# Early rows of w_up: the last two products exchanged, the spilled first product as one fp32 tile, and pools at 256-byte steps

## The chip, the cores and the metric

The kernel runs on one core of a Trainium2 chip. The metric is the device time of one execution, in microseconds; lower is better. TensorE does the matrix products, ACT (ScalarE) and DVE (VectorE) move results from PSUM to SBUF and do elementwise work, POOL (GpSimd) does small work and issues DMAs, and SP (SyncE) only issues DMAs.

## The reference

One decoder layer on 1024 tokens of width 1024, in float32: parallel token mixers, cross-attention to 256 memory tokens, and a gated MLP with a causal convolution of width 3. The change touches the first half of the MLP, and the places of tiles everywhere.

```python
h += W_out(g_A * P_A(n) + g_B * P_B(n))            # n = RMSNorm(h)
h += CrossAttn(RMSNorm(h), RMSNorm(mem))
h += W_down(silu(conv(u)_gate) * conv(u)_val)      # u = W_up RMSNorm(h), 2816 + 2816 columns
```

## The kernel before

A product of high precision is made of three fp32r products: each operand is split into a rounded part (hi) and its rest (lo), and hi x hi, hi x lo and lo x hi are summed in PSUM (`mm3`, L97). The split is one ACT copy and one DVE subtraction (`split_to`, L81; `hilo`, L103, from PSUM).

u = W_up n is computed for 22 rows of 128 columns, each a gate half and a value half, for the two halves of the tokens. One row is a 2 x 2 block product by Strassen's scheme in Winograd's form, seven products in place of eight. A product (`product`, L812) is four blocks of 128 times three, twelve matmuls of 128 x 512. The right operands are "11", "21" and "22" and the sums t1 to t4, all split once; the left operands are a row's weights w1 and w2 (raw tiles wr and w), of which only l22 is used as it is, and the sums s1 to s4, made on DVE by `sum_weights` (L920) and split into tiles mh and ml with two buffers each.

A row is made by three functions. `up_start` (L895) allocates ug and uv (gate and value rows before the convolution; tag hu, two buffers, so each row takes the buffers of the row before), opens bank A and puts the first product into it. `up_middle` (L936) adds s2 x t2 to A and copies it out (U2, L948), makes s3 x t3 in bank B, adds s1 x t1 to A and copies that out (U4, L953), and writes B plus U4 into the second half of uv. `up_end` (L956) has the last two products: c12, s4 x R22 added to A, which is then copied to ug (L958); and c21, l22 x t4 added to B, which is written with U2 into the first half of uv (L960). `add_into` (L916) is an ACT copy (L917) and a DMA on POOL's queue that adds a tile in place (L918). Then both rows go through the convolution (ACT L966, DVE L967 and L968), SiLU and product; of odd rows, six halves and sums are written to r_d for the last stage.

The rows stand in a pipeline: for each g, `up_start(g)`, `up_end(g - 1)`, `up_middle(g)`. Ten of the 22 rows are early rows (NEARLY = 10): their products with "11" and "21" are made beforehand by `up_early` (L827), since only the first half of the tokens is needed for them. It makes the first product P1, stores it as a split pair in er_d, adds the second and stores the sum in e_d. Row g then loads the pair by two DMAs on POOL's queue (L904, L905) and puts both into bank A with an identity matrix in fp32r (`ident_r`, copied at L166; L906, L907); the stored sum is loaded straight into the first half of ug by SP (L940). The other twelve rows, the late rows, make all seven products in place.

Each engine's order of work is set by a planner in the framework: it goes through the instructions by the time it believes them ready, and the order of the text is the tie-break. Engines work through their own order one after the other; POOL's and SP's DMAs are issued in theirs.

Tiles live in pools: cp, bp and the tag pools (ug, uv, y, h, weights wr, wh, wl, activations a2h, a2l, and the e tiles that `etile` takes) on the left, ap, xp, mp, tp and dn on the right of SBUF. The tiles neghalf and ident_r (cp), rs8 (L168), rsm (L699) and ncw (L1087) have widths that set where the others begin.

Of the kernel before, what the change touches and what calls it, by code (L numbers as in the profile page):

```python
# [7 lines left out]
F32 = mybir.dt.float32  # L8
F32R = mybir.dt.float32r
AF = mybir.ActivationFunctionType  # L10
# [4 lines left out]
P = 128  # L15
T = 1024
D = 1024
NK = D // P
HT = 512
# [17 lines left out]
NEARLY = 10  # L37
# [5 lines left out]
def hybrid_layer(ctx: ExitStack, tc: tile.TileContext, x, xT, mem, memT, w_in, w_v, w_br, w_out, w_xq, w_xk, w_xv, w_xo, w_up,  # L43
                 w_down, vecs, ln_f, consts, tabs, out):
    nc = tc.nc

    cp = ctx.enter_context(tc.tile_pool(name="cp", bufs=1))
# [3 lines left out]

    ident = cp.tile([P, P], F32, name="ident")
    vec = cp.tile([P, V_N], F32, name="vec")
    neghalf = cp.tile([P, 16], F32, name="neghalf")
    ident_r = cp.tile([P, P + 16], F32R, name="ident_r")[:, :P]

    ga_d = dp.tile([16, P, T], F32, name="ga_d")
    yt_d = dp.tile([6, P, T], F32, name="yt_d")
# [1 line left out]
    rs_d = dp.tile([T], F32, name="rs_d")  # L60
    sd_d = dp.tile([NF // 2, P, 4, HT], F32, name="sd_d")
    r_d = dp.tile([NF // 2, 7, P, HT], F32, name="r_d")
    e_d = dp.tile([NEARLY, P, HT], F32, name="e_d")
    er_d = dp.tile([NEARLY, 2, P, HT], F32R, name="er_d")
    h_d = dp.tile([8, P, D], F32, name="h_d")

    def f(ap):
# [35 lines left out]
    def hilo(hi, lo, ps, scale=None):  # L103
        if scale is None:
            nc.scalar.activation(hi, ps, AF.Copy)
            nc.vector.tensor_tensor(lo, ps, f(hi), op=ALU.subtract)
        else:
            nc.scalar.activation(hi, ps, AF.Copy, scale=scale)
            nc.vector.scalar_tensor_tensor(lo, ps, scale, f(hi), op0=ALU.mult, op1=ALU.subtract)
# [53 lines left out]
            hilo(nT[h][0][:, k], nT[h][1][:, k], xt[:, h * HT:(h + 1) * HT], vec[:, V_MIX + k:V_MIX + k + 1])  # L163

    nc.sync.dma_start(ident, consts[:, 0:P])
    nc.scalar.activation(ident_r, ident, AF.Copy)  # L166
    nc.sync.dma_start(cst, consts[:, P:])
    rs8 = ap.tile([P, 16], F32, name="rs8")[:, 0:8]  # L168
    for t in range(8):
        xk = ap.tile([P, D], F32, tag="kg", name="xk", bufs=4)  # L170
        nc.sync.dma_start(xk, x[t * P:(t + 1) * P, :])
# [497 lines left out]
    def etile(name, dt=F32):  # L669
        return ep.tile([P, HT], dt, tag="e", name=name, bufs=7)  # L670
# [17 lines left out]
    def mem_prep():  # L688
        KT = KV["k"] = (slot([P, 4, MEM], F32R, "kth"), slot([P, 4, MEM], F32R, "ktl"))
        VM = KV["v"] = (slot([P, 2, HT], F32R, "vmh"), slot([P, 2, HT], F32R, "vml"))  # L690
        mh = [slot([P, 4, MEM], F32R, "mh") for _ in range(2)]
        ml = [slot([P, 4, MEM], F32R, "ml") for _ in range(2)]
        for c in range(2):
            mr = slot([P, 4, MEM], F32, "mr")
            nc.gpsimd.dma_start(mr, memT[c])
            for kk in range(4):
                g = V_MEM + 4 * c + kk
                hilo(mh[c][:, kk], ml[c][:, kk], mr[:, kk], vec[:, g:g + 1])
        rsm = xp.tile([P, 18], F32, name="rsm")[:, :2]  # L699
        for t in range(2):  # L700
            mt = slot([P, D], F32, "mt")
            nc.gpsimd.dma_start(mt, mem[t * P:(t + 1) * P, :])
            nc.scalar.activation(mt, mt, AF.Square, accum_out=rsm[:, t:t + 1])
        nc.vector.tensor_scalar(rsm, rsm, 1.0 / D, EPS, op0=ALU.mult, op1=ALU.add)
        rstd(rsm, 2)
        rbm = slot([P, MEM], F32, "rbm")
        nc.vector.tensor_copy(rbm, row_bcast(rsm, 2)[:, :MEM])
        KV["m"] = mh, ml, rsm, rbm
# [103 lines left out]
    def product(ps, w, r, first):  # L812
        for kk in range(4):
            ks = slice(kk * P, (kk + 1) * P)
            mm3(ps, (w[0][:, ks], w[1][:, ks]), (r[0][:, kk], r[1][:, kk]), first and kk == 0, kk == 3,
                skip_group_check=True)
# [4 lines left out]
    R = {}  # L821
# [5 lines left out]
    def up_early(gs):  # L827
        ps = {}
        for g in gs:
            ps[g] = bank("mm", 3, "pe"), *gate_weights(g)  # L830
            product(ps[g][0], ps[g][1], R["11"], True)
            hi, lo = etile("phi", F32R), etile("plo", F32R)
            hilo(hi, lo, ps[g][0])
            nc.gpsimd.dma_start(er_d[g, 0], hi)
            nc.gpsimd.dma_start(er_d[g, 1], lo)
        for g in gs:
            product(ps[g][0], ps[g][2], R["21"], False)
            c11 = etile("c11")
            nc.scalar.activation(c11, ps[g][0], AF.Copy)
            nc.gpsimd.dma_start(e_d[g], c11)  # L840

    def spill_h(t):
        nc.gpsimd.dma_start(h_d[t], h[t])
# [51 lines left out]
    def up_start(g):  # L895
        u = {}
        u["ug"], u["uv"] = (htile([P, 2 + T + 14], "hu", n) for n in ("ug", "uv"))
        u["A"] = bank("zz", 2, "pA")
        u["w1"] = raw_w(w_up[g])
        u["w2"] = htile([P, 2 * HT], "hr", "w2")  # L900
        nc.sync.dma_start(u["w2"], w_up[NF + g])
        if g < NEARLY:
            hi, lo = etile("phi", F32R), etile("plo", F32R)
            nc.gpsimd.dma_start(hi, er_d[g, 0])  # L904
            nc.gpsimd.dma_start(lo, er_d[g, 1])  # L905
            nc.tensor.matmul(u["A"], ident_r, hi, start=True, stop=False, skip_group_check=True)  # L906
            nc.tensor.matmul(u["A"], ident_r, lo, start=False, stop=True, skip_group_check=True)  # L907
        else:
            hi, lo = split(u["w1"])
            u["l12"] = hi[:, HT:], lo[:, HT:]  # L910
            product(u["A"], (hi[:, :HT], lo[:, :HT]), R["11"], True)
            u["p1"] = etile("p1")
            nc.scalar.activation(u["p1"], u["A"], AF.Copy)
        return u

    def add_into(dst, ps, x):  # L916
        nc.scalar.activation(dst, ps, AF.Copy)  # L917
        nc.gpsimd.dma_start(dst, x, accum_op=ALU.add)  # L918
# [17 lines left out]
    def up_middle(g, u):  # L936
        for n in ("ug", "uv"):
            nc.gpsimd.memset(u[n][:, 0:2], 0.0)
        if g < NEARLY:
            nc.sync.dma_start(u["ug"][:, 2:2 + HT], e_d[g])  # L940
        else:
            d = bank("mm", 3, "pD")
            product(d, u["l12"], R["21"], True)
            add_into(u["ug"][:, 2:2 + HT], d, u["p1"])
        s1, s2, s3, u["s4"] = sum_weights(u)
        product(u["A"], s2, R["t2"], False)
        u["U2"] = etile("U2")
        nc.scalar.activation(u["U2"], u["A"], AF.Copy)  # L948
        u["B"] = bank("tr", 2, "pB")
        product(u["B"], s3, R["t3"], True)  # L950
        product(u["A"], s1, R["t1"], False)
        u4 = etile("U4")
        nc.scalar.activation(u4, u["A"], AF.Copy)  # L953
        add_into(u["uv"][:, 2 + HT:2 + T], u["B"], u4)

    def up_end(g, u):  # L956
        product(u["A"], u["s4"], R["22"], False)
        nc.scalar.activation(u["ug"][:, 2 + HT:2 + T], u["A"], AF.Copy)  # L958
        product(u["B"], u["l22"], R["t4"], False)
        add_into(u["uv"][:, 2:2 + HT], u["B"], u["U2"])  # L960
        ys = []
        for n, cw, cb, sign in (("ug", vec, V_CB + g, 0), ("uv", ncw, V_CB + NF + g, 1)):
            c0 = 3 * g if sign else V_CW + 3 * g
# [120 lines left out]
    mp = ctx.enter_context(tc.tile_pool(name="mp", bufs=1, side="right"))  # L1084
    ts_ = ExitStack()
    tp_ = ts_.enter_context(tc.tile_pool(name="tp", bufs=1, side="right"))
    ncw = mp.tile([P, 160], F32, name="ncw")  # L1087
    nc.vector.tensor_scalar(ncw[:, :3 * NF], vec[:, V_CW + 3 * NF:V_CW + 6 * NF], -1.0, None, op0=ALU.mult)
    right_sums(b12, b22)
    before = None  # L1090
# [89 lines left out]
```

## Time and profile before

| | us |
|---|---|
| median of three runs | 1780.95 |
| lowest and highest | 1777.82 and 1784.14 |
| the profiled execution | 1780.45 |
| its span | 1778.6 |
| TensorE busy | 1693.4 |
| DVE busy | 1113.0 |
| ACT busy | 871.0 |
| POOL busy | 326.9 |

The profile is one execution; its mean granted TensorE clock is 0.986 of full speed. The engine rows overlap, so they do not add up to the span. `up_early` and the set-up of the right operands end near 1149 us; the early rows run until about 1298 us, the late rows until 1550, the last stage until the end. Matmuls overlap in the records, so the distance between starts tells the pace better than a matmul's own length.

### The profile page before, as it was taken

How to read it: one execution, taken by the hardware profiler on the slowest of the kernel's cores; microseconds unless marked ns; L12 is line 12 of the kernel's file. 1: busy time of each engine (PE TensorE's matmuls, PEld its weight loads, DVE VectorE, ACT ScalarE, POOL GpSimd, SP SyncE). 2: the span in 40 equal slices, each digit the busy share in tenths (PEclk: the TensorE clock that was granted, in tenths of full speed). 3: DMA queues.
4: the chain of work that ended last, by engine and by line, in shares of the span. 5: the costliest groups of instructions: out<-in, count | busy, mean ns of one | idle time of the engine just before them, and what ended most of it. 6: DMA issues, size and time to landing. Idle time of an engine off the chain costs nothing.

```text
span 1778.6 us, 23614 instructions
## 1 busy us (share of the span) xinstructions
PE 1693.4 (95%) x8598; PEld 1378.1 (77%) x8598; DVE 1113.0 (63%) x1737; ACT 871.0 (49%) x1495; POOL 326.9 (18%) x511
## 2 busy tenths in 40 slices
PE   7999999998999899999999989798999999989997
PEld 5977777878878787788888767576778888778885
DVE  3764654468757466575645666777777767655556
ACT  5344544466345445444534455454555555534344
POOL 0442333221112110001000102222222222200002
PEclk9999999999999999999999999899999999999999
DMA  7443333455774843566322325666755454677664
GB/s 305 113 123 92 107 83 84 134 134 145 200 140 118 159 113 95 180 181 249 131 95 72 130 83 178 206 165 184 211 148 157 136 136 125 188 259 231 214 191 140
DMA packets 106388, 273.01 MB, mean 153 GB/s; under 512 B 16096, under 2 KB 16352, under 8 KB 106272
## 3 DMA queue, kind: packets, MB, share of 16 engines
q1 hardware_dynamic: 66368, 166.68, 28.9%
q0 software_dynamic: 39904, 104.82, 24.1%
q8 instruction: 68, 1.11, 0.3%
q14 instruction: 48, 0.39, 0.1%
HBM read 188.77 MB, written 74.29 MB: 148 GB/s over the span
## 4 chain that ended last, share of the span: by engine, by line
PE 66%; issue 13%; DMA 10%; DVE 5%; ACT 3%; POOL 3%; SPq 0%; POOLq 0%; DVEq 0%; ACTq 0%
PE mm L99 4%; PE mm L101 4%; PE mm L100 4%; PE pA L99 3%; PE pA L100 3%; PE pA L101 3%; DMA sd_d<-in_w_down_dram 2%; DMA uv<-U 2%; PE mmt L99 2%; PE dA L100 2%; PE dA L101 2%; PE mmt L100 2%; PE mmt L101 2%; PE dA L99 2%; DMA xw<-xs 2%
## 5 line engine op out<-in xcount | busy, mean ns | idle before, releaser
L101 PE MATMUL mm<-a2h,wl 128*128 128x512 f32 x592 | 235.2, 398 | 0.0
L99 PE MATMUL mm<-a2h,wh 128*128 128x512 f32 x592 | 234.7, 396 | 0.0
L100 PE MATMUL mm<-a2l,wh 128*128 128x512 f32 x592 | 234.5, 396 | 0.0
L83 DVE TENSOR_TENSOR wl<-wr,wh 128x1024 fp32r<-128x1024 f32 (+1 forms) x119 | 145.3, 1222 | 95.0 <-ACT wh L82 92.1
L82 ACT ACTIVATE wh<-wr 128x1024 fp32r<-128x1024 f32 (+1 forms) x119 | 124.0, 1043 | 132.6 <-PE mmt L101 29.2
L83 DVE TENSOR_TENSOR dl<-rl,dh 128x1024 fp32r<-128x1024 f32 x77 | 94.1, 1224 | 85.0 <-ACT dh L82 81.5
L82 ACT ACTIVATE dh<-rl 128x1024 fp32r<-128x1024 f32 x77 | 81.2, 1058 | 114.6 <-PE dA L101 41.2
L101 PEld LDWEIGHTS mm<-a2h,wl 128*128 128x128 f32 x592 | 112.4, 190 | 22.2 <-issue 1.0
L100 PEld LDWEIGHTS mm<-a2l,wh 128*128 128x128 f32 x592 | 112.3, 190 | 22.3 <-issue 0.9
L99 PEld LDWEIGHTS mm<-a2h,wh 128*128 128x128 f32 x592 | 112.5, 190 | 22.0 <-issue 0.9
L493 DVE TENSOR_TENSOR_SCAN kp<-kp 128x128 f32<-128x128 f32 (+7 forms) x64 | 86.8, 1356 | 29.4 <-ACT kp L490 29.1
L99 PE MATMUL pA<-a2h,mh 128*128 128x512 f32 x176 | 70.5, 400 | 14.9 <-ACT U L953 14.9
L502 ACT ACTIVATE at<-tra 128x512 f32<-128x512 f32 (+3 forms) x96 | 43.3, 489 | 76.9 <-PE tra L500 59.6
L112 POOL TENSOR_TENSOR ss<-ss,neghalf 128x1 f32<-128x1 f32 x24 | 23.3, 995 | 307.6 <-DVE ss L597 305.7
L490 ACT ACTIVATE kp<-zz,zsc 128x512 f32<-128x512 f32 (+3 forms) x96 | 55.6, 583 | 49.3 <-DVE zz L489 44.5
L381 ACT ACTIVATE sp<-sp,nm 128x128 f32<-128x128 f32 (+1 forms) x96 | 42.3, 442 | 72.6 <-DVE nm L379 72.5
L100 PE MATMUL dA<-dl,dh 128*128 128x512 f32 x176 | 70.1, 398 | 3.5 <-DVE dl L83 3.5
L101 PE MATMUL dA<-dh,dl 128*128 128x512 f32 x176 | 70.0, 397 | 0.0
L101 PE MATMUL pA<-a2h,ml 128*128 128x512 f32 x176 | 69.3, 394 | 0.0
L100 PE MATMUL pA<-a2l,mh 128*128 128x512 f32 x176 | 69.3, 394 | 0.0
L99 PE MATMUL dA<-dh 128*128 128x512 f32 x176 | 62.1, 393 | 3.8 <-ACT dh L82 3.8
L491 ACT ACTIVATE gg<-zz,zsc 128x512 f32<-128x512 f32 (+3 forms) x96 | 55.7, 583 | 7.1 <-DVE gg L494 7.1
(352 smaller groups left out, 4587.4 us busy)
## 6 DMA issues: line engine op xcount, KB each, us to landing
rl<-r_d SPq DMA_DIRECT2D x77, 256.0 KB, 3.2
wr<-in_w_in_dram SPq DMA_DIRECT2D x37, 512.0 KB, 4.2
wr<-in_w_up_dram SPq DMA_DIRECT2D x32, 512.0 KB, 4.3
w<-in_w_up_dram SPq DMA_DIRECT2D x22, 512.0 KB, 3.7
uv<-U POOLq DMA_DIRECT2D x44, 256.0 KB, 4.7
r_d<-ts POOLq DMA_DIRECT2D x44, 256.0 KB, 4.8
rl<-sd_d SPq DMA_DIRECT2D x44, 256.0 KB, 3.6
r_d<-y POOLq DMA_DIRECT2D x33, 256.0 KB, 3.4
```

What stands on the lines that cost most here:

```text
L82: nc.scalar.activation(hi, raw, AF.Copy)
L83: nc.vector.tensor_tensor(lo, raw, f(hi), op=ALU.subtract)
L99: nc.tensor.matmul(ps, wh, rh, start=first, stop=False, **kw)
L100: nc.tensor.matmul(ps, wh, ro, start=False, stop=False, **kw)
L101: nc.tensor.matmul(ps, wo, rh, start=False, stop=last, **kw)
L112: nc.gpsimd.tensor_tensor(ss, ss, neghalf[:, :n], op=ALU.pow)
L381: nc.scalar.activation(sp[:, a, :n], sp[:, a, :n], AF.Exp, scale=0.125, bias=nm[:, a:a + 1], accum_out=ost[:, 130 + a:131 + a])
L490: nc.scalar.activation(kp[:, c0:c1], z[:, :n], AF.Sigmoid, scale=zsc[:, 1, i:i + 1])
L491: nc.scalar.activation(gg[:, c0:c1], z[:, :n], AF.Sigmoid, scale=zsc[:, 0, i:i + 1])
L493: nc.vector.tensor_tensor_scan(rev, rev, rev, 1.0, op0=ALU.mult, op1=ALU.bypass)
L502: nc.scalar.activation(s[:, :nb * P], tp[:, :nb * P], AF.Copy)
```

## The change

- In `up_end`, c21 and its evacuation stand before c12 and its evacuation as long as the next row is an early row (g + 1 < 10).
- `up_early` stores P1 as one fp32 tile (one ACT copy, one DMA on POOL's queue). Row g loads it by one DMA on SP's queue and puts it into bank A with one fp32 matmul with `ident`. `ident_r` and its copy go, and er_d becomes a second plane of e_d.
- neghalf, rs8, rsm and ncw get wider by 16 or 32 elements.

```diff
--- before.py
+++ after.py
@@ -51,8 +51,7 @@
 
     ident = cp.tile([P, P], F32, name="ident")
     vec = cp.tile([P, V_N], F32, name="vec")
-    neghalf = cp.tile([P, 16], F32, name="neghalf")
-    ident_r = cp.tile([P, P + 16], F32R, name="ident_r")[:, :P]
+    neghalf = cp.tile([P, 32], F32, name="neghalf")
 
     ga_d = dp.tile([16, P, T], F32, name="ga_d")
     yt_d = dp.tile([6, P, T], F32, name="yt_d")
@@ -60,8 +59,7 @@
     rs_d = dp.tile([T], F32, name="rs_d")
     sd_d = dp.tile([NF // 2, P, 4, HT], F32, name="sd_d")
     r_d = dp.tile([NF // 2, 7, P, HT], F32, name="r_d")
-    e_d = dp.tile([NEARLY, P, HT], F32, name="e_d")
-    er_d = dp.tile([NEARLY, 2, P, HT], F32R, name="er_d")
+    e_d = dp.tile([NEARLY, 2, P, HT], F32, name="e_d")
     h_d = dp.tile([8, P, D], F32, name="h_d")
 
     def f(ap):
@@ -163,9 +161,8 @@
             hilo(nT[h][0][:, k], nT[h][1][:, k], xt[:, h * HT:(h + 1) * HT], vec[:, V_MIX + k:V_MIX + k + 1])
 
     nc.sync.dma_start(ident, consts[:, 0:P])
-    nc.scalar.activation(ident_r, ident, AF.Copy)
     nc.sync.dma_start(cst, consts[:, P:])
-    rs8 = ap.tile([P, 16], F32, name="rs8")[:, 0:8]
+    rs8 = ap.tile([P, 48], F32, name="rs8")[:, 0:8]
     for t in range(8):
         xk = ap.tile([P, D], F32, tag="kg", name="xk", bufs=4)
         nc.sync.dma_start(xk, x[t * P:(t + 1) * P, :])
@@ -696,7 +693,7 @@
             for kk in range(4):
                 g = V_MEM + 4 * c + kk
                 hilo(mh[c][:, kk], ml[c][:, kk], mr[:, kk], vec[:, g:g + 1])
-        rsm = xp.tile([P, 18], F32, name="rsm")[:, :2]
+        rsm = xp.tile([P, 50], F32, name="rsm")[:, :2]
         for t in range(2):
             mt = slot([P, D], F32, "mt")
             nc.gpsimd.dma_start(mt, mem[t * P:(t + 1) * P, :])
@@ -829,15 +826,14 @@
         for g in gs:
             ps[g] = bank("mm", 3, "pe"), *gate_weights(g)
             product(ps[g][0], ps[g][1], R["11"], True)
-            hi, lo = etile("phi", F32R), etile("plo", F32R)
-            hilo(hi, lo, ps[g][0])
-            nc.gpsimd.dma_start(er_d[g, 0], hi)
-            nc.gpsimd.dma_start(er_d[g, 1], lo)
+            p1 = etile("p1")
+            nc.scalar.activation(p1, ps[g][0], AF.Copy)
+            nc.gpsimd.dma_start(e_d[g, 0], p1)
         for g in gs:
             product(ps[g][0], ps[g][2], R["21"], False)
             c11 = etile("c11")
             nc.scalar.activation(c11, ps[g][0], AF.Copy)
-            nc.gpsimd.dma_start(e_d[g], c11)
+            nc.gpsimd.dma_start(e_d[g, 1], c11)
 
     def spill_h(t):
         nc.gpsimd.dma_start(h_d[t], h[t])
@@ -900,11 +896,9 @@
         u["w2"] = htile([P, 2 * HT], "hr", "w2")
         nc.sync.dma_start(u["w2"], w_up[NF + g])
         if g < NEARLY:
-            hi, lo = etile("phi", F32R), etile("plo", F32R)
-            nc.gpsimd.dma_start(hi, er_d[g, 0])
-            nc.gpsimd.dma_start(lo, er_d[g, 1])
-            nc.tensor.matmul(u["A"], ident_r, hi, start=True, stop=False, skip_group_check=True)
-            nc.tensor.matmul(u["A"], ident_r, lo, start=False, stop=True, skip_group_check=True)
+            p1 = etile("p1")
+            nc.sync.dma_start(p1, e_d[g, 0])
+            nc.tensor.matmul(u["A"], ident, p1, start=True, stop=True, skip_group_check=True)
         else:
             hi, lo = split(u["w1"])
             u["l12"] = hi[:, HT:], lo[:, HT:]
@@ -937,7 +931,7 @@
         for n in ("ug", "uv"):
             nc.gpsimd.memset(u[n][:, 0:2], 0.0)
         if g < NEARLY:
-            nc.sync.dma_start(u["ug"][:, 2:2 + HT], e_d[g])
+            nc.sync.dma_start(u["ug"][:, 2:2 + HT], e_d[g, 1])
         else:
             d = bank("mm", 3, "pD")
             product(d, u["l12"], R["21"], True)
@@ -954,10 +948,16 @@
         add_into(u["uv"][:, 2 + HT:2 + T], u["B"], u4)
 
     def up_end(g, u):
-        product(u["A"], u["s4"], R["22"], False)
-        nc.scalar.activation(u["ug"][:, 2 + HT:2 + T], u["A"], AF.Copy)
-        product(u["B"], u["l22"], R["t4"], False)
-        add_into(u["uv"][:, 2:2 + HT], u["B"], u["U2"])
+        def c12():
+            product(u["A"], u["s4"], R["22"], False)
+            nc.scalar.activation(u["ug"][:, 2 + HT:2 + T], u["A"], AF.Copy)
+
+        def c21():
+            product(u["B"], u["l22"], R["t4"], False)
+            add_into(u["uv"][:, 2:2 + HT], u["B"], u["U2"])
+
+        for part in (c21, c12) if g + 1 < NEARLY else (c12, c21):
+            part()
         ys = []
         for n, cw, cb, sign in (("ug", vec, V_CB + g, 0), ("uv", ncw, V_CB + NF + g, 1)):
             c0 = 3 * g if sign else V_CW + 3 * g
@@ -1084,7 +1084,7 @@
     mp = ctx.enter_context(tc.tile_pool(name="mp", bufs=1, side="right"))
     ts_ = ExitStack()
     tp_ = ts_.enter_context(tc.tile_pool(name="tp", bufs=1, side="right"))
-    ncw = mp.tile([P, 160], F32, name="ncw")
+    ncw = mp.tile([P, 192], F32, name="ncw")
     nc.vector.tensor_scalar(ncw[:, :3 * NF], vec[:, V_CW + 3 * NF:V_CW + 6 * NF], -1.0, None, op0=ALU.mult)
     right_sums(b12, b22)
     before = None
```

## Rows read from the trace of the kernel before

**Rows 1.** Windows, early and late rows: length, busy time by engine (instructions), clock, DMA share, GB/s.
```profile
1164.50:1297.50 133.00, 118.13 (x496) 93.55 (x495) 100.42 (x109) 72.63 (x90) 38.77 (x75) 0.99 0.66 189
...
1303.00:1545.00 242.00, 242.00 (x1053) 197.37 (x1052) 177.68 (x183) 133.82 (x173) 59.28 (x106) 1.00 0.52 139
```
**Rows 2.** Waits, 1148 to 1303 us: us in total, times, longest.
```profile
ACT y L966 <- DMA uv<-U: 15.1, 7, 3.9
...
PE pA L99 <- ACT U L953: 14.9, 8, 3.2
...
DVE wr L924 <- DMA wr<-in_w_up_dram: 13.1, 6, 3.5
```
**Rows 3.** Timeline, TensorE, first matmuls of c12: start, us, idle before in brackets.
```profile
1174.89 0.50 PE L99 MATMUL pA<-a2h,mh 128*128 128x512 f32 x1 [1.41 <-ACT U L953]
...
1207.55 0.50 PE L99 MATMUL pA<-a2h,mh 128*128 128x512 f32 x1 [2.05 <-ACT U L953]
...
1292.13 0.50 PE L99 MATMUL pA<-a2h,mh 128*128 128x512 f32 x1 [1.41 <-ACT U L953]
```
**Rows 4.** Timeline, ACT, early row 3.
```profile
1204.83 1.24 ACT L966 ACTIVATE y<-uv,vec,ncw 128x1024 f32<-128x1024 f32 x1 [3.31 <-DMA uv<-U]
...
1205.98 1.04 ACT L82 ACTIVATE mh<-w 128x1024 fp32r<-128x1024 f32 x1
...
1206.92 0.57 ACT L953 ACTIVATE U<-pA 128x512 f32<-128x512 f32 x1
...
1208.88 0.60 ACT L917 ACTIVATE uv<-pB 128x512 f32<-128x512 f32 x1 [1.38 <-DVE y L968]
```
**Rows 5.** Timeline, TensorE: last matmul of row 0, then last ones of three t1 products.
```profile
1164.30 0.39 PE L101 MATMUL pA<-a2h,ml 128*128 128x512 f32 x1
...
1173.10 0.39 PE L101 MATMUL pA<-a2h,ml 128*128 128x512 f32 x1
...
1205.11 0.39 PE L101 MATMUL pA<-a2h,ml 128*128 128x512 f32 x1
...
1290.34 0.39 PE L101 MATMUL pA<-a2h,ml 128*128 128x512 f32 x1
```
**Rows 6.** Timeline, DVE: last convolution step of uv in early rows.
```profile
1172.52 1.28 DVE L968 SCALAR_TENSOR_TENSOR y<-uv,ncw,y 128x1024 f32<-128x1024 f32 x1
...
1207.48 1.28 DVE L968 SCALAR_TENSOR_TENSOR y<-uv,ncw,y 128x1024 f32<-128x1024 f32 x1
...
1291.39 1.28 DVE L968 SCALAR_TENSOR_TENSOR y<-uv,ncw,y 128x1024 f32<-128x1024 f32 x1
```
**Rows 7.** Timeline, POOL, early row 2.
```profile
1195.39 0.71 POOL L990 DMA_DIRECT2D r_d<-ts  x1
...
1197.93 0.89 POOL L918 DMA_DIRECT2D uv<-U  x1 [1.83 <-DVE y L967]
```
**Rows 8.** Timeline at 710.6 us, and grouped lines from 705 to 715 us: fp32 products.
```profile
710.61 1.52 PE L507 MATMUL avs<-at,v 128*64 128x128 f32 x22
...
L507 PE MATMUL avs<-at,v 128*64 128x128 f32 x24 | 2.0, 279 | 0.0
```
**Rows 9.** Timeline, TensorE: the end of the early first products.
```profile
1141.96 0.56 PE L99 MATMUL pe<-a2h,wh 128*128 128x512 f32 x1 [1.81 <-DVE plo L106]
...
1148.54 0.50 PE L99 MATMUL pB<-t3h,mh 128*128 128x512 f32 x1 [1.96 <-ACT mh L82]
```
**Rows 10.** Grouped lines, TensorE, late rows (1303 to 1545 us): count, busy us, mean ns.
```profile
L101 PE MATMUL pA<-a2h,ml 128*128 128x512 f32 x101 | 39.4, 390 | 0.0
...
L101 PE MATMUL pB<-t4h,wl 128*128 128x512 f32 x52 | 20.5, 395 | 0.0
```
**Rows 11.** Timeline, TensorE, late rows: first matmuls of three products in a row.
```profile
1408.64 0.40 PE L99 MATMUL pB<-t4h,wh 128*128 128x512 f32 x1
...
1411.43 0.39 PE L99 MATMUL pA<-a2h,mh 128*128 128x512 f32 x1
...
1414.17 0.40 PE L99 MATMUL pA<-t2h,mh 128*128 128x512 f32 x1
```

## Prediction

> **What bounds the kernel now.** I read the page's busy shares and its 40 slices first: TensorE is the busiest engine, in nearly every slice, so a gain has to come from its idle time, from fewer or shorter matmuls, or from a higher granted clock. The windows come next, to see where the idle time lies. In the early rows of w_up (from the identity matmul of row 1 to that of row 9, eight rows) TensorE works 118.13 of 133.00 us, and 14.87 us are idle; in the late rows it is busy for all of 242.00 us [rows 1]. So an exchange in the early rows can win at most about 15 us, and the late rows can only win if each matmul becomes shorter. In both windows the granted clock is 0.99 to 1.00, the 2.4 GHz level.
>
> Then the waits of the early rows [rows 2]. TensorE's idle time there is one wait, repeated in eight rows: c12 (bank A, weights s4) waits for the ACT copy U4 at L953, 14.9 us in all. Its ACT instruction is late because ACT was itself waiting for the DMA add into uv (15.1 us). The timeline shows the single stalls: 1.41 us in five rows, 2.05, 3.16 and 2.62 us in rows 3, 5 and 7; the first, third and last of the eight stand in [rows 3]. Row 3 shows the mechanism [rows 4]: ACT sits 3.31 us in L966 on the landing of uv, then runs a weight copy (L82), then L953, and only then may c12 start. The last matmul of the product with t1 had begun at 1205.11 [rows 5], c12 at 1207.55.
>
> A second chain ends still later. uv and ug of two consecutive rows share buffers, so the evacuation of bank B (L917) must wait until the last convolution step L968 has read the uv of the row before. That step ends 0.4 us after the product with t1 in row 1 (1172.52 + 1.28 against 1173.10 + 0.23), 3.4 us in row 3 and 2.1 us in row 8 [rows 5, 6]; the whole series is 0.4, 1.5, 3.4, 2.1, 4.5, 1.7, 4.0 and 2.1, mean 2.5. Now c12 hides most of it: c12 needs bank A only, c21 needs bank B.
>
> **Exchange of c12 and c21.** It removes nothing; it moves c21 with its evacuation L917 and its DMA add (POOL, L918) ahead of c12. One product is twelve matmuls of 242.00/1053 = 0.23 us [rows 1], 2.76 us. So the uv chain (L917, add, L966, L967, L968) starts 2.76 us earlier, and its end, taken against the next row's product with t1, which the fp32 identity makes 0.44 us later (below), moves by 3.2 us in rows 2 to 8. In row 1 it gains 0.44 only, because the planner already ran row 0 with c12 last: the matmul before the second identity matmul at 1164.53 is an A product [rows 5]. But c21 can't start before L917, about 0.8 us after L968 (0.60 and the hand-over). Measured start to start, today's stalls are 0.16 longer than the idle time, 14.9 + 8 x 0.16 = 16.2 us. What remains is the lateness less the shift plus 0.8, not below zero. With the shift taken cautiously as 2.3, since SP's and POOL's transfers share the engines, rows 1 to 8 give 0.8, 0, 1.9, 0.6, 3.0, 0.2, 2.5 and 0.6, together 9.6. The gain is 6.6; I take **-6.5**. Bounds: -14.9 if every wait goes, and a loss (rival C) if uv does not land earlier. Queues: the add is moved past c12's copy L958 on ACT, and on POOL it comes among the r_d issues that odd rows leave; in row 2 the last of these (L990) stands at 1195.39 and the add at 1197.93 [rows 7]. Behind a waiting L917 on ACT stand the split of the next weights and L958. The split of w1's sums (L82, 1.04 us [rows 4], then its second half on DVE) is released only after c12, so now one product later, with the identity and the product with t2 (3.66 us) as cover; without that cover the 1.04 us and as much again would show in each row.
>
> **One fp32 identity instead of two fp32r ones.** It removes a matmul of 0.23 us, SP takes one load instead of POOL two, and 256 KB per row leave the DMA engines. The trace has no fp32 matmul of 512 columns. The nearest row is the avs product, fp32, 128 columns moved: 22 records in 1.52 us [rows 8], of which 0.28 is the last one's own length; (1.52 - 0.28)/22 = 0.056 each. Two records make one product on one half of the array, so a product over the full width and 512 columns is 4 x 2 x 2 x 0.056 = 0.90 us, if the halves do not overlap further. Bounds: 0.46 (what the two cost now) and 1.10 (the tail counted in). I take 0.90: 0.44 more per row, on the path, ten rows: **+4.4** (0 to +6.4).
>
> **Early first products.** In up_early the DVE half of the split (L106) and one of two POOL issues go. Today the last half product starts at 1141.96, after 1.81 us on that DVE step; the first product with t3 then starts at 1148.54, after 1.96 us on a weight copy of ACT [rows 9]. ACT's copy alone, which comes first in the split today, is done earlier, so the 1.81 go. The weight copy behind them is queued on ACT after one that waits for this product's buffer, so it comes forward as well, until the landing of w_up holds it. If both waits go, 3.8 us are won, if the landing holds everything, nothing. The last half product stands right behind the DVE step, so I lean to the upper end: **-2.8**.
>
> **Pads.** They move the right-hand pools by 128 bytes, the left-hand ones by 512. Added up from the tiles, t2, t3 and t4 start at 0 modulo 256 today, while the weights mh, wh and the activations a2h start at 128; afterwards all agree modulo 256. In the late rows the page's mean duration is 390 ns where moving and stationary operand agree (a2h with mh) and 395 ns where they differ by 128 (t4 with wh) [rows 10]. The timeline confirms it start to start: twelve matmuls of t4 take 2.79 us (1408.64 to 1411.43), the following twelve of a2h 2.74 (to 1414.17) [rows 11], so 4 ns per matmul. I count some 1430 mismatched matmuls of 512 columns: 36 in each of 22 rows, the rest with w0, the branch products, xo's left operand and pv. About 1110 of them lie outside the eight early rows, 4.4 us, and 288 inside, 1.2, of which the waits there swallow half: **-5.0**, bounds -6.5 and 0.
> A rule speaks against this term. The Trainium skill, "TensorE: Matmul & The Clock Gate", section "Step-by-step: what each phase is for", says that weight loading and the moving operand have separate read ports of SBUF, and that loading the next weights takes no bandwidth from the running matmul. By it where the two operands lie could not matter, and the sum would be 5.0 higher; [rows 10, 11] speak for the address.
>
> **Sum.** It is made against the profiled execution, 1780.45 us (span 1778.6), which is 0.5 below the median of the three runs (1780.95). 1780.45 - 6.5 + 4.4 - 2.8 - 5.0 = **1770.5 us**.
>
> **Rivals.**
> B: the exchange is not made. The planner orders each engine by what it believes ready, and took c21 first in row 0 without being told to [rows 5]. If c12 is ready first by its reckoning, it keeps c12 first whatever the text says; for this speaks that ACT runs L953 ahead of L917 at the stalls [rows 2, 4]. Then the waits stay: 1780.45 + 4.4 - 2.8 - 5.6 = 1776.4.
> C, slower: the chain of uv does not move with c21. Its add is issued on POOL among the r_d writes, and in DVE's order L968 stands behind an L924 that waits for its load (13.1 us in six rows) [rows 2, 7]. If L968 ends as late as now, c21 waits 2.5 + 0.8 - 0.44 = 2.84 us per row with nothing to cover it, 22.7 us in place of 16.2; with one us more in the four rows whose add meets the r_d issues it is 26.7. That gives 1780.45 + 6.5 (to 10.5) + 4.4 - 2.8 - 4.4 = 1784 to 1788. It decides against the change from a mean wait of 2.4 us per row on. Against it: in most rows the releaser of ACT is the add itself, which starts with c21.
> D: all early waits go: 1780.45 - 14.9 + 4.4 - 2.8 - 5.8 = 1761.4.
> E: addresses do nothing, and the 5 ns belong to what the t products share otherwise (their place between evacuations): 1770.5 + 5.0 = 1775.5. In [rows 10] the two groups have the same shape, type and stretch, so this is less likely. The rule of the Trainium skill named under the pads would give this case.
>
> **How the numbers follow.** Forecast 0.42, B 0.22, C 0.15, D 0.08, E 0.13. About 0.3%, 5.3 us, is what can be told from no change, so faster means below 1775.6. Faster: most of the forecast (0.36), D (0.08), a third of B and half of E (0.13), together 0.57. Slower: nearly all of C, 0.14. Same: 0.29. Range: it reaches from D's end at 1761 to the middle of C, 1786, with the unknown costs of the forecast (1761 to 1780) inside.
>
> **What would show it.** Exchange right: the product with t4 stands before the one with R22 in the early rows, the wait on L953 is gone, and a smaller one on the ACT copy of bank B (L917) stands in its place, mainly in rows 3, 5 and 7. Wrong: c12 still first, or a wait on L917 of over 2.4 us per row. Identity: its two records start and the next product starts 0.90 later. Early stage: the first product with t3 begins near 1145.7 of the clock of before. Pads: t2, t3, t4 and a2h products all at about 390 ns, and the late rows, 14 of them with 36 such matmuls each, 2 us shorter. The prediction falls if the uv add lands later than now, if the fp32 product costs over 1.1 us, or if the pads change nothing.

## The result and the profile after

The changed kernel takes 1769.14 us (median of four runs, 1767.94 to 1770.45) against 1779.65 for the kernel before beside it: the ratio is 0.9937, with a 95% interval of 0.9916 to 0.9958. Measured again, beside later variants, it gave 1768.51 against 1780.03, 0.9939 (0.9925 to 0.9952). The forecast was 1770.5, so the total came out as foretold. Its terms did not: one of them is zero, and two others were little more than half of what the runs showed.

Lines of `kernel.py` shift by a few with the change: `mm3` is L97 to L99 after (L99 to L101 before), the weight copy L80 (L82), the evacuation of bank B L911 (L917), U4's copy L947 (L953), the identity L901.

First the windows of the changed kernel (length, busy time by engine with instructions, clock, DMA share, GB/s), the early rows 1 to 8 and the late rows, to be held against [rows 1].

```profile
1156.57:1289.35 132.78, 118.51 (x490) 92.08 (x489) 100.64 (x108) 71.07 (x88) 29.73 (x59) 0.99 0.60 173
1300.00:1515.00 215.00, 215.00 (x950) 178.11 (x949) 162.41 (x170) 121.56 (x157) 54.46 (x99) 1.00 0.52 140
```

The eight early rows last 132.78 us in place of 133.00, with 490 matmuls in place of 496, since the identity of row 9 now stands inside c12 of row 8; TensorE is idle for 14.27 us in place of 14.87. The term from which I expected 6.5 us is not there. In the late rows a matmul takes 215.00/950 = 0.226 us in place of 0.230.

The waits of the changed kernel from 1085 to 1303 us (us in total, times, longest), beside [rows 2]:

```profile
ACT y L966 <- DMA uv<-U: 17.1, 8, 4.6
...
DVE wr L918 <- DMA wr<-in_w_up_dram: 10.2, 4, 4.0
...
PE pB L97 <- ACT uv L911: 9.9, 5, 4.5
...
PE pA L97 <- ACT U L947: 4.2, 3, 1.4
```

The wait on U4 is left in three rows, and in five rows a wait on the copy of bank B stands in its place, up to 4.5 us long. So c21 does come first in some rows. The timeline of TensorE (start, us, idle before in brackets) shows both orders, in row 1 and in row 4, beside [rows 3]:

```profile
1166.74 0.50 PE L97 MATMUL pB<-t4h,wh 128*128 128x512 f32 x1 [0.95 <-ACT uv L911]
...
1169.59 0.39 PE L97 MATMUL pA<-a2h,mh 128*128 128x512 f32 x1
...
1214.64 0.50 PE L97 MATMUL pA<-a2h,mh 128*128 128x512 f32 x1 [1.41 <-ACT U L947]
...
1218.59 0.40 PE L97 MATMUL pB<-t4h,wh 128*128 128x512 f32 x1
```

In row 1 c21 (t4) runs before c12 (a2h with mh). In row 4 c12 runs first, and c21 only at 1218.59, behind the identity of row 5. Going through the whole order, c21 is first in rows 0, 1, 2, 3, 6 and 8, and c12 in rows 4, 5 and 7.

The identity, timeline of TensorE, beside [rows 8]:

```profile
1156.57 1.02 PE L901 MATMUL pA<-p,ident 128*128 128x512 f32 x2
1157.02 0.80 PE L97 MATMUL pA<-t2h,mh 128*128 128x512 f32 x1
1157.66 0.40 PE L98 MATMUL pA<-t2l,mh 128*128 128x512 f32 x1
```

From its start to the start of the second matmul of t2, less one matmul of 0.23, are 0.86 us; I had taken 0.90.

The end of the set-up, beside [rows 9], again the timeline of TensorE:

```profile
1136.79 0.50 PE L97 MATMUL pe<-a2h,wh 128*128 128x512 f32 x1 [0.69 <-ACT p L830]
...
1141.95 0.50 PE L97 MATMUL pB<-t3h,mh 128*128 128x512 f32 x1 [2.15 <-ACT mh L80]
```

The first product with t3 starts at 1141.95, 6.6 us before the 1148.54 of before; I had expected 2.8. And the pads, grouped lines of TensorE in the late rows (count, busy us, mean ns), beside [rows 10]:

```profile
L99 PE MATMUL pA<-a2h,ml 128*128 128x512 f32 x92 | 35.8, 389 | 0.0
...
L99 PE MATMUL pB<-t4h,wl 128*128 128x512 f32 x44 | 17.1, 389 | 0.0
```

Both groups now show 389 ns; before, t4 had 395.

### The profile page after: what moved, and what is told of

It is laid out like the page before. It is cut to its first block, busy times and chain, and to the rows that moved or that the text cites. A ratio compares the mean times of both kernels' runs of the same rounds, so it can differ in the third digit from the quotient of the medians.

```text
span 1767.2 us, 23575 instructions
## 1 busy us (share of the span) xinstructions
PE 1684.1 (95%) x8598; PEld 1374.3 (78%) x8598; DVE 1108.3 (63%) x1727; ACT 871.9 (49%) x1494; POOL 310.5 (18%) x481
## 4 chain that ended last, share of the span: by engine, by line
PE 42%; DVE 3%; DMA 3%; ACT 2%; issue 1%; POOL 0%; SPq 0%; POOLq 0%; ACTq 0%; DVEq 0%
PE pA L97 3%; PE pA L98 3%; PE pA L99 3%; DMA uv<-U 2%; PE dA L98 2%; PE mmt L97 2%; PE dA L99 2%; PE mmt L98 2%; PE dA L97 2%; PE mmt L99 2%; PE pB L97 2%; PE pB L98 2%; PE dB L99 2%; PE dB L97 2%; PE dB L98 2%; PE pB L99 2%
## 5 line engine op out<-in xcount | busy, mean ns | idle before, releaser
L99 PE MATMUL mm<-a2h,wl 128*128 128x512 f32 x592 | 234.2, 396 | 0.0
L98 PE MATMUL mm<-a2l,wh 128*128 128x512 f32 x592 | 233.7, 395 | 0.0
L97 PE MATMUL mm<-a2h,wh 128*128 128x512 f32 x592 | 233.6, 395 | 0.0
L80 ACT ACTIVATE wh<-wr 128x1024 fp32r<-128x1024 f32 (+1 forms) x119 | 124.0, 1043 | 134.0 <-PE mmt L99 28.8
L80 ACT ACTIVATE dh<-rl 128x1024 fp32r<-128x1024 f32 x77 | 81.2, 1059 | 113.2 <-PE dA L99 34.5
L99 PEld LDWEIGHTS mm<-a2h,wl 128*128 128x128 f32 x592 | 111.9, 189 | 22.1 <-issue 1.0
L97 PEld LDWEIGHTS mm<-a2h,wh 128*128 128x128 f32 x592 | 111.9, 189 | 21.9 <-issue 0.9
L97 PE MATMUL pA<-a2h,mh 128*128 128x512 f32 x176 | 69.0, 392 | 4.4 <-ACT U L947 4.2
L99 PE MATMUL dA<-dh,dl 128*128 128x512 f32 x176 | 70.2, 399 | 0.0
L99 PE MATMUL pA<-a2h,ml 128*128 128x512 f32 x176 | 68.6, 390 | 0.0
L97 PE MATMUL dA<-dh 128*128 128x512 f32 x176 | 61.6, 391 | 3.8 <-ACT dh L80 3.8
```

The lines of the kernel that those rows point to most:

```text
L80: nc.scalar.activation(hi, raw, AF.Copy)
L97: nc.tensor.matmul(ps, wh, rh, start=first, stop=False, **kw)
L98: nc.tensor.matmul(ps, wh, ro, start=False, stop=False, **kw)
L99: nc.tensor.matmul(ps, wo, rh, start=False, stop=last, **kw)
```

## The experiments

The runs were made in three groups (e1 to e4, e5 to e8, e9 to e11), each on a chip of its own and beside runs of the kernel before, so between groups the ratios are compared and not the times. For the comparison of stages I use one window, from the first product with t3 (the start of row 0) to the first matmul of the last stage. It holds the 22 rows of w_up but for their last 58 matmuls, which follow it in every run; it is called the 22 rows below.

One thing has to be read beside it. TensorE's granted clock falls from its 2.4 GHz level to 1.2 GHz for short stretches, and not for the same ones in each run. In row 5 of the kernel before it fell behind a wait of 3.16 us:

```profile
1241.34 0.79 PE L99 MATMUL pA<-a2h,mh 128*128 128x512 f32 x1 [3.16 <-ACT U L953]
1241.93 0.63 PE L100 MATMUL pA<-a2l,mh 128*128 128x512 f32 x1
1242.36 0.63 PE L101 MATMUL pA<-a2h,ml 128*128 128x512 f32 x1
1242.79 0.63 PE L99 MATMUL pA<-a2h,mh 128*128 128x512 f32 x1
```

The last three start 0.43 us apart, in place of 0.23. The changed kernel was profiled twice with the same order on every engine, and its 22 rows stood at the 1.2 GHz level for 3.4 us in the first trace and for 10.2 us in the second:

```profile
1141.95:1521.00 379.05, 364.78 (x1571) 295.33 (x1571) 283.08 (x299) 206.67 (x265) 89.80 (x164) 1.00 0.55 154
```

```profile
1140.00:1521.67 381.67, 367.60 (x1570) 297.38 (x1571) 283.10 (x299) 206.67 (x265) 89.79 (x164) 0.99 0.54 153
```

So single traces of one kernel differ by 2.6 us here, and about half of the time at the low level has to be taken off before two of them are compared (an estimate from 0.43 against 0.23 us a matmul). In the 22 rows it is 6.8 us for the kernel before, e1 and e4, 3.4 for e2 and e7, 10.2 for e3 and e8, 9.6 for e6, and none for e5, e10 and e11.

**One part at a time.** The pads alone, the single fp32 tile alone, and the exchange alone.

```diff
 # e1_pads, on the kernel before
-    rs8 = ap.tile([P, 16], F32, name="rs8")[:, 0:8]
+    rs8 = ap.tile([P, 48], F32, name="rs8")[:, 0:8]
-        rsm = xp.tile([P, 18], F32, name="rsm")[:, :2]
+        rsm = xp.tile([P, 50], F32, name="rsm")[:, :2]
-    ncw = mp.tile([P, 160], F32, name="ncw")
+    ncw = mp.tile([P, 192], F32, name="ncw")
```

> The kernel before with the widths of rs8, rsm and ncw alone (the right-hand pools move by 128 bytes, so that t2, t3, t4, w0, the branch products' and xo's operands agree modulo 256 with the weights on the left). The order of every engine stays that of before. Theory (addresses): the matmuls of t2, t3 and t4 go from about 232 to 227 ns start to start, the late rows get 2 to 4 us shorter, and the whole 4 to 7 us faster, about 1774. Rival (separate read ports, addresses do nothing): pace unchanged, 1780, and what the changed kernel won comes from the single fp32 tile.

Measured: 1774.55 us, ratio 0.9955 (0.9938 to 0.9972), 8 us faster. The same two groups in its late rows:

```profile
L101 PE MATMUL pA<-a2h,ml 128*128 128x512 f32 x90 | 35.0, 389 | 0.0
...
L101 PE MATMUL pB<-t4h,wl 128*128 128x512 f32 x44 | 17.1, 389 | 0.0
```

Start to start, the groups with t2, t3 and t4 go from means between 230.7 and 233.7 ns to 226.6 to 228.1; the products with w0 from 233.3 to 227, those of the branches from 232 to 227. Products whose own operands had agreed before gain too, where a neighbour had not (a2h with mh from 228.7 to 227.0). The 22 rows take 377.17 us in place of 382.16, with the idle time unchanged and as long at the low clock:

```profile
1151.93:1529.10 377.17, 362.09 (x1570) 296.43 (x1571) 281.35 (x297) 204.51 (x263) 98.95 (x181) 0.99 0.58 161
```

The window of the kernel before:

```profile
1148.54:1530.70 382.16, 367.29 (x1570) 296.63 (x1571) 280.52 (x296) 204.99 (x263) 98.94 (x181) 0.99 0.57 158
```

The last stage gains as well, 244.9 in place of 247.9 us. Its two operands come by turns from a pool that moved and one that did not, which may be why; I had left it out of my count. So the theory of the addresses holds, and it was worth more than I took.

```diff
 # e2_p1: the changed kernel with the old widths of rs8, rsm and ncw, and
-        for part in (c21, c12) if g + 1 < NEARLY else (c12, c21):
+        for part in (c12, c21):
```

> The single fp32 tile with its fp32 identity alone (old pads on the right, c12 before c21 in the text). Theory now, after the trace of the changed kernel: the set-up stage ends 6 to 7 us earlier, the early rows take as long as before (shorter waits, but 0.4 us more of identity per row), so 4 to 6 us faster, about 1775; in some early rows c21 stands before c12 although the text says otherwise. Rival (the forecast's terms): set-up 2.8 us earlier, early rows 4.4 us longer, so 1.6 us slower, about 1781.5.

Measured: 1781.57 us, ratio 0.9991 (0.9977 to 1.0005): no difference that can be measured. By stages it wins and loses: from the first early product to the first product with t3 are 119.4 us in place of 124.1 (125.0 in the run with the exchange alone), so 5 us less, and the 22 rows take 383.30 in place of 382.16, although they stood at the low clock for 3.4 us less. The planner's order of all engines is the same as in the changed kernel, with c21 first in rows 0, 1, 2, 3, 6 and 8, although its text has c12 first.

```diff
 # e3_exchange: the kernel before, with up_end as in the changed kernel
+        for part in (c21, c12) if g + 1 < NEARLY else (c12, c21):
+            part()
```

> The exchange in the text alone. Rival B of the prediction (the planner keeps its own order): order and time as before, 1780, within 0.2%, and TensorE's idle time in the early rows again 14.9 us. Forecast: c21 ahead of c12 in rows 1 to 8, waits of 9 to 10 us in place of 16, about 6.5 us faster, 1773.5.

Measured: 1783.51 us, ratio 1.0002 (0.9986 to 1.0018). Every engine has the same instructions in the same order as before. Its waits from 1153 to 1309 us:

```profile
PE pA L99 <- ACT U L953: 13.9, 8, 3.0
```

This is the wait of before, in eight rows. Rival B holds: the exchange in the text does nothing. What put c21 ahead in some rows of the changed kernel is the other edit, the single fp32 tile, by which the planner reckons other times: the run before this one has that order with c12 first in the text. Which part of that edit does it (the load on SP, the one copy or the one identity) was not tried.

**c21 truly first.** Does the forecast's mechanism work at all, where the order is made?

```diff
 # e4_pinned, on the changed kernel: the first matmul of c12 is tied behind the last of c21
-            product(u["A"], u["s4"], R["22"], False)
+            product(u["A"], u["s4"], R["22"], False, pin=g + 1 < NEARLY)
 # in mm3
+        m = nc.tensor.matmul(ps, wh, rh, start=first, stop=False, **kw)
+        if pin:
+            tc.keep_in_program_order(m)
```

> The changed kernel, and the first matmul of c12 pinned behind the last of c21 in the early rows, so that c21 does run first in every row. Theory of the forecast (uv's chain moves with c21): the long waits of rows 5, 6 and 8 shrink and it is 3 to 6 us faster than the changed kernel, about 1764. Rival C (the chain stays, and nothing covers the wait for bank B): 5 to 12 us slower than the changed kernel, 1774 to 1781.

Measured: 1770.57 us, ratio 0.9938 (0.992 to 0.9957), as the changed kernel; neither theory. Its waits from 1150 to 1300 us:

```profile
PE pA L903 <- DMA p<-e_d: 9.7, 5, 2.3
...
ACT y L968 <- DMA uv<-U: 3.7, 3, 1.9
...
PE pB L97 <- ACT uv L913: 2.9, 3, 1.3
```

ACT's wait for uv falls from 17.1 to 3.7 us, and those of TensorE on copies of the banks from 14.1 to 2.9. This part of the mechanism is right: uv's chain moves with c21. But a new wait of 9.7 us has come: the identity of the next row waits for its fp32 tile. SP's queue shows why (timeline, row 8):

```profile
1282.92 0.33 SPq L936 DMA_DIRECT2D ug<-e_d  x1
...
1283.41 0.33 SPq L902 DMA_DIRECT2D p<-e_d  x1
...
1286.26 0.95 PE L903 MATMUL pA<-p,ident 128*128 128x512 f32 x1 [1.95 <-DMA p<-e_d]
```

The load stands on SP behind the load into ug, which has to wait for the buffer that the row before still uses. It is issued only 2.85 us before the identity starts, which waits 1.95 us for it.

**The load one row ahead.** Two runs, pinned and not.

```diff
 # e5_pin_ahead on e4_pinned, e6_ahead on the changed kernel: in up_middle, ahead of ug's load
+        if g + 1 < NEARLY:
+            P1[g + 1] = load_p1(g + 1)    # makes the tile and loads it on SP's queue
 # in up_start
-            p1 = etile("p1")
-            nc.sync.dma_start(p1, e_d[g, 0])
+            p1 = P1.pop(g) if g in P1 else load_p1(g)
```

> The kernel pinned as in the run before (c21 ahead of c12 in the early rows), and each row's fp32 tile loaded one row ahead, before the load of ug on SP's queue. The pinned run waited 2.9 us for bank B and 9.7 us for that load, which stood behind the load into the shared ug. Theory: the loads were the last thing in the way; early rows without waits of either kind, 8 to 10 us less than the changed kernel, about 1760. Rival (the DMA engines are full there, or the planner's new order puts another wait in its place): within 3 us of the changed kernel, 1767 to 1772.

> The changed kernel with the load one row ahead, nothing pinned; by the planner's order c12 then stands ahead of c21 again, with two matmuls of the next row's first product ahead of both. Theory (the waits come from U4's copy in ACT's order, and c21 behind c12 makes the chain of uv late): waits of 8 to 14 us stay, 1766 to 1770. Rival (where the load comes early, the order of c12 and c21 does not matter): as fast as the pinned one with the load ahead.

Measured: 1765.78 us, ratio 0.9892 (0.9875 to 0.991), and 1768.45, ratio 0.9913 (0.9897 to 0.9929), side by side. The pinned one is ahead, but gains less than I had put down (1765.8 for 1760), and the intervals of the two overlap. Its granted clock was 0.989 in the mean of its runs against 0.986 for the other, which by estimate (0.003 of 1765 us) makes 5 us, more than the 2.7 between them. So it is not shown that the order adds anything to the load ahead, unless by way of the clock. The waits of the pinned one from 1150 to 1300 us, and its 22 rows:

```profile
PE pA L97 <- ACT mh L80: 6.4, 7, 0.9
...
ACT y L976 <- DMA uv<-U: 5.2, 6, 1.6
...
PE pB L97 <- ACT uv L919: 2.0, 8, 0.4
```

```profile
1146.18:1519.49 373.31, 364.83 (x1570) 293.66 (x1571) 283.37 (x299) 206.28 (x265) 89.75 (x164) 1.00 0.56 155
```

The same of the one that is not pinned:

```profile
ACT y L974 <- DMA uv<-U: 20.1, 8, 4.5
...
PE pA L97 <- ACT mh L80: 9.5, 8, 2.7
```

```profile
1148.99:1527.32 378.33, 367.98 (x1571) 296.54 (x1571) 282.16 (x299) 206.10 (x265) 89.67 (x164) 0.99 0.55 153
```

In the pinned one the wait for the load is gone, and 8.5 us of idle time stay, most of it on a split of weights. The planner had put two matmuls of the next product with t2 ahead of c21, and they wait for weights which ACT can copy only once the product with t1 is done. The rows of the pinned one are 5.7 and 8.4 us shorter than in the two traces of the changed kernel, some 3 to 4 us with the clock taken off. But this cannot be put down to c21 being first. Without the pin c12 is first again in rows 1 to 8 and ACT waits 20.1 us for uv, and still the idle time is only 1.9 us more (10.35 against 8.48); the rows are 5.0 us longer, with 9.6 us at the low clock against none, so by the same estimate they are as long without it. What both have is the load ahead, and the rival of the second run stands.

**Is it the address?** Two looks, with other places.

```diff
 # e7_left_128, on the kernel before
-    neghalf = cp.tile([P, 16], F32, name="neghalf")
+    neghalf = cp.tile([P, 48], F32, name="neghalf")
 # e8_tp_64, on the changed kernel
-    ncw = mp.tile([P, 192], F32, name="ncw")
+    ncw = mp.tile([P, 176], F32, name="ncw")
```

> The kernel before with the left-hand pools moved by 128 bytes in place of the right-hand ones (neghalf 32 elements wider): wh and a2h now start at 0 modulo 256 like t4, while mh stays at 128. Theory (agreement of the two operands modulo 256 counts, not the place itself): t4 with wh goes from 232 to 227 or 228 ns start to start, t2 and t3 with mh stay at 232, and a2h with mh, which now differ, rises from 228 to about 232. Rival (128 modulo 256 is the good place): nothing improves, and a2h with wh gets slower.

> The changed kernel with ncw 16 elements narrower: t2, t3 and t4 start at 192 modulo 256, 64 bytes off mh and wh at 128. Theory (only a multiple of 256 is free of it): their matmuls take 231 to 235 ns in place of 227, the late rows 2 to 3 us longer than in the changed kernel. Rival (only an offset of 128 hurts): 227 ns as in the changed kernel.

Grouped lines of TensorE in the late rows of the first, with the left pools at 0 modulo 256:

```profile
L101 PE MATMUL pA<-a2h,ml 128*128 128x512 f32 x92 | 36.2, 393 | 0.0
...
L101 PE MATMUL pB<-t3h,ml 128*128 128x512 f32 x46 | 18.2, 395 | 0.0
...
L101 PE MATMUL pB<-t4h,wl 128*128 128x512 f32 x44 | 17.2, 391 | 0.0
```

and of the second, with t2 to t4 64 bytes off:

```profile
L99 PE MATMUL pA<-a2h,ml 128*128 128x512 f32 x90 | 35.2, 391 | 0.0
...
L99 PE MATMUL pB<-t3h,ml 128*128 128x512 f32 x44 | 17.4, 395 | 0.0
...
L99 PE MATMUL pB<-t4h,wl 128*128 128x512 f32 x44 | 17.3, 392 | 0.0
```

In the first, t4 with wh, which agree now, goes from 231.7 to 233.2 ns start to start to 227.0 to 228.2; t3 with mh stays at 233 to 235, and a2h with mh, which no longer agree, rises from 228.7 to 233. So no place is good in itself: the two operands must lie a multiple of 256 bytes apart. In the second, t2 and t3 stand at 230.4 to 231.0, between the 227 of agreement and the 232 of 128 bytes, and the three groups of t4 at 228.5 to 232.5. From the first product with t3 of row 10 to that of row 21, where the clock is full in both, it takes 211.92 us against 208.99 in the changed kernel, 2.9 more, as the theory had it. This was one execution each; the pace of some fifty to ninety matmuls in each group is what carries it, and not the total.

**What the identity costs, and the last wait.** The changed kernel once more, and two variants of the pinned kernel with the load ahead: one with a single fp32r pass as identity, which leaves out the low part of the first product, and one with t2's product pinned behind c12.

```diff
 # e10_one_pass, on e5_pin_ahead (p1 is an fp32r tile, ident_r an fp32r copy of ident)
-            nc.tensor.matmul(u["A"], ident, p1, start=True, stop=True, skip_group_check=True)
+            nc.tensor.matmul(u["A"], ident_r, p1, start=True, stop=True, skip_group_check=True)
 # e11_pin_t2, on e5_pin_ahead
-        product(u["A"], s2, R["t2"], False)
+        product(u["A"], s2, R["t2"], False, pin=0 < g < NEARLY)
```

> The changed kernel once more, beside the two variants that build on it, so that they stand on the same chip. Expected 11 us below the kernel before (0.993 to 0.995). Its early rows are expected to wait for the copies of banks A and B as in its first trace, 14 us.

> The pinned kernel with the load one row ahead, whose identity product is one fp32r pass in place of fp32: the low part of the first product is left out, to price the fp32 identity where almost no wait can hide it. Theory (it costs 0.63 us more than one pass, ten rows, on the path): 5 to 6 us faster than the pinned kernel with the load ahead, about 1760. Rival (it lies in a wait): within 2 us of it, 1765.

> The pinned kernel with the load one row ahead, and the product with t2 of the next row pinned behind c12, so that c21 follows the product with t1 directly. Before, two matmuls of t2 stood there and waited 0.92 us for the split of their weights, and c21 0.24 us for bank B. Theory (the split was the only thing waited for): up to 1.2 us per row less in eight rows, 1757 to 1762. Rival (then bank B is not ready and c21 waits for L917 as long): as the pinned kernel with the load ahead, 1764 to 1767.

Measured: 1768.51 us, ratio 0.9939 (0.9925 to 0.9952); 1758.99, ratio 0.9885 (0.9871 to 0.9899); 1756.76, ratio 0.9872 (0.9853 to 0.9891). The 22 rows of the last two, in this order:

```profile
1139.60:1507.60 368.00, 358.52 (x1561) 291.59 (x1561) 282.93 (x299) 206.27 (x265) 89.61 (x164) 1.00 0.56 158
```

```profile
1136.17:1506.60 370.43, 362.94 (x1570) 294.24 (x1571) 283.55 (x299) 206.65 (x265) 89.91 (x164) 1.00 0.56 156
```

With one pass in place of the fp32 identity TensorE's busy time in the 22 rows falls by 6.3 us (364.83 to 358.52), which is ten times the 0.86 - 0.23 = 0.63 of the start distances, and the rows are 5.3 us shorter (368.00 against 373.31). Both traces have the full clock there. So the identity lies on the path once the waits are small. The times do not tell the two apart (0.9885 against 0.9892 in the other group, with intervals that overlap), so its price rests on these rows. With t2 pinned, the only wait left in the early rows is on bank B:

```profile
PE pB L97 <- ACT uv L919: 7.5, 8, 1.5
```

It comes to 7.5 us in eight rows, up to 1.5 us in one. The split of the weights was hidden, and the rival partly holds: bank B is ready about a microsecond too late. Still, the rows are 2.9 us shorter than in the pinned kernel with the load ahead. This kernel beats both the kernel before and the changed one: 1756.76 us, 1.3% below the first and some 12 us below the second beside it. Its granted clock was 0.989 in the mean of its runs against 0.986 for the changed kernel, so by estimate (0.003 of 1760 us) 5 to 6 of the 12 us are the clock. In the early rows of all traces every fall of the clock comes behind a wait of TensorE, and the three runs with the shortest waits there (0.9, 1.1 and 1.5 us at most, in e5, e10 and e11) show no fall; that the shorter waits keep the clock up is likely, and was not tried by itself.

## Why the prediction was right, and where not

**The total** was right: 1770.5 foretold, 1769.14 measured, faster as foretold. **The terms** make it partly by luck: the 6.5 us that the exchange did not bring were made up by 3 us more from the pads, about 2 more from the set-up and an identity that cost less than the 4.4 us.

**Exchange, foretold -6.5: it measured 0** (1.0002, with the order of every engine unchanged). The step that failed is the first sentence of that term, that the edit moves c21. The order of the text does not decide where one of the two is ready first by the planner's reckoning. Rival B said just this, from c21 standing first in row 0 untold and from L953 ahead of L917 at the stalls, and I gave it 0.22; it should have been the likeliest. That uv's chain moves with c21 was right: with c21 held first, ACT's wait for uv fell from 17.1 to 3.7 us. That this is worth 6.5 us was not: the time stayed where it was (0.9938 against 0.9937), and with the load ahead the rows are as long with c12 first as with c21 first, the clock apart; whether the pin keeps the clock up is open. What I did not see is what is late next, the load behind SP's load into ug and then a split of weights. The prediction asked which queue the add passes, but not which queue the new SP load joins.

**Identity, foretold +4.4.** The length was right, 0.86 us for 0.90, so 0.40 per row more than the two passes. On the path it came to less: the 22 rows with the single tile alone are 1.1 us longer than before, and by estimate 2.8 with the clock taken off (3.4 us at the low level in place of 6.8). The idle time of the eight early rows fell from 14.87 to 13.24 us beside it, with c21 first in some of them. Where the waits are gone it counts nearly in full (5.3 us for ten times 0.63).

**Set-up, foretold -2.8: it measured about -5** with the tile alone, and -7 in the changed kernel, of which up to 2 are the clock (10.2 us of the set-up at the low level, against 13.7 before and with the tile alone). I had looked at the last wait only. Before, the waits from 1085 to 1149 us were

```profile
PE pe L101 <- DVE wl L83: 5.6, 1, 5.6
...
PE pe L99 <- DVE plo L106: 2.4, 2, 1.8
```

and with the tile alone, from 1094 to 1149 us,

```profile
PE pe L97 <- ACT p L830: 1.7, 3, 0.7
PE pe L99 <- DVE wl L81: 0.7, 1, 0.7
```

The long wait was on a weight split, which stood behind ten operations that DVE ran without a break from 1109.28 us on. None of the low halves is among the ten; two of them, 0.7 us each, ran ahead. With the tile alone the planner put DVE's work in another order, and the longest such wait is 0.7 us. Whether the removed work or the new order took the 5 us away is not shown.

**Pads, foretold -5.0: they measured -8.0** (-5.0 to -11.1 by timing; by stages -5 in the 22 rows, -3 in the last stage and up to 1 in the set-up). The sign and the mechanism were right, the 4 ns per matmul were about 5, and the neighbours and the last stage were not in the count. The sign of being right in the late rows counts 14 of them where there are 12; from row 10 to row 21 they became 3.3 us shorter (214.77 to 211.48, at the full clock), for the 2 foretold. The rule of the Trainium skill, "TensorE: Matmul & The Clock Gate", section "Step-by-step: what each phase is for", by which weight loading takes nothing from the running matmul, gave rival E, in which the place of the operands could not matter. It does: 227 against 232 ns for operands a multiple of 256 apart and 128 off. Rival E falls. Whether the loading of weights is what takes the 5 ns, against the rule, was not shown.

**Sum of the parts.** Pads alone -8, tile alone -1.6 (-4.1 to +0.9), exchange 0: together -9.6, against -11 for the whole, within the intervals. Rivals C and D did not come. C's price could not be seen, since pinning c21 first made the chain earlier and not later.

What stays open: the tile alone wins 5 us in the set-up and loses 1 in the rows, and the last stage has 1 less, so its stages say about -5; its timing says -1.6, with an interval that ends at -4.1. The time from the start to the first early product varies between 1021 and 1033 us in the profiles (1024.4 before, 1029.1 with the tile alone); the cause is open.

## What to carry to other kernels

Before costing a change of order in the text, ask whether the planner follows the text there: compare the order of the engines, and where it must hold, tie the instruction. When a wait is moved away, look at the queue that the new or moved load joins, and load ahead of whatever waits for a buffer there. Let the moving and the stationary operand of matmuls that follow one another start a multiple of 256 bytes apart; a few padding elements were worth 0.45% here. Read the granted clock beside every difference between two single traces.

## What the runs showed of the hardware

The pace of a matmul of 128 x 512 in fp32r hangs on the distance of its operands in SBUF: 227 to 228 ns where they lie a multiple of 256 bytes apart, 228.5 to 232.5 at 64 bytes off, and 231 to 235 at 128 off. It does not matter which of the two moved.

A product with agreeing operands behind one with others is slow at first and recovers. In the kernel before, the first three of the twelve matmuls of a2h with mh, behind products with t3 or t4, take 230.5 to 232.5 ns and the last two 226.6 to 226.8; with the pads alone all twelve take 226 to 227. This would fit the loading of weights beside the running matmul; that this is the cause was not shown.

At the 1.2 GHz level such a matmul takes 427 ns.
